# Attention phase of a two-layer encoder step: sinks as a kept PSUM column, first loads in another order, output products one step sooner, values stored by halves

## Chip, cores and metric

The kernel runs on one core of one Trainium2 chip. The metric is the device time of one launch in microseconds (us), as the median of several runs. A profiled execution gives the trace that all durations below come from. The engines are called PE (matrix multiplications), PEld (its weight loads), DVE (vector), ACT (scalar functions), POOL (the fourth compute engine) and SP (which here only issues DMAs).

## Reference

2048 prompt tokens and 32 sampled tokens of width 1024 go through a DeltaNet layer, then through a layer of sliding-window attention with learned sinks. Only the second one is touched by the change, apart from an order of columns.

```python
def sink_softmax(s, sinks):
    sk = sinks.astype(jnp.float32)[..., None, None]
    m = jnp.maximum(s.max(-1, keepdims=True), sk)
    p = jnp.exp(s - m)
    return p / (p.sum(-1, keepdims=True) + jnp.exp(sk - m))

def swa_layer(x, k, v, pos, cached, w_in, sinks, w_out, ln_g, ln_b):
    proj = x @ w_in
    q = rope_partial(proj[..., :B_QW].reshape(b, l, B_Q_HEADS, B_HD), pos) * (B_HD ** -0.5)
    q = q.reshape(b, l, B_KV_HEADS, B_GROUP, B_HD)
    z = proj[..., B_QW:]
    ...
    # 16 query heads, 4 key heads, head size 64; a 64-token chunk sees itself and the two chunks before it
    o = banded_attention(q, k, v, sk)          # scores, sink_softmax, times values
    out = (o * jax.nn.silu(z)) @ w_out
    return layer_norm(DN_ALPHA * x + out, ln_g, ln_b)
```

## The kernel before

The first 1747 us of the trace are the DeltaNet layer, the shared keys and values, and the query and gate projections of the second layer. Large matrix products in fp32 are done as three products of a high and a low part (L79 to L81 for the projections, L1117 to L1119 for the output product: 24 matmuls for half the columns of 128 tokens).

The last 420 us are `Attention.run`. Its instructions stand on PE, DVE, ACT, POOL and SP in the order in which the code writes them (`manual_schedule`), and an engine takes them strictly in that order. `run` goes over the 64-token chunks in the order 14 to 31, then 0 to 13, and then the sampled tokens; i counts the places in that order (0 to 31, `last` = 32 for the sampled ones). Each chunk has two groups of heads, p = 0 and 1. One iteration i does on PE:

- `values(i)`: the probabilities of chunk i times the values, into two PSUM banks (L1701);
- `score(i+2, 0)`: scores of the chunk after next into a PSUM tile S (L1660);
- `turn(i+1, 0)`: transposes of probabilities into the PSUM tile tr (L1683);
- half the output product of the 128-token tile `po` (two chunks make a tile; c says which half of the columns);
- `turn(i+1, 1)` and `score(i+2, 1)`.

The output product uses the banks of `values`, so `values(i+1)` needs the bank that `added` (DVE L1125: residual r plus product) empties. The softmax of one (i, p) is a chain across engines: the largest score (DVE L1480), the sink joined to it (DVE L1483), the sink's difference (DVE L1493), four exps with their sums (ACT L1490) and one of the sink (ACT L1494), the total (DVE L1497), its reciprocal (DVE L1500) and the shares (POOL L1504, two operations in place). ACT (L1689) and DVE (L1690) copy the transposed tile out, and `gated` (DVE L1712) multiplies the result by the gate zs into graw.

A finished tile goes through `finish` (load of the residual r, L1511), `cast` (ACT L1518), `rest` (POOL L1522: the low part), its two products, `stats` (DVE L1538), `norm` (DVE: L1543, L1546, then Newton steps for the inverse root, L484, L487 and three times L491, L493, L495, then L1551), `normed` (ACT L1554), `affine` (POOL L1558 and L1559, 128x1024 each) and `store`. `step(n)` takes n instructions of the norm that is under way and puts them at that place on DVE.

Before the loop and in iterations 0 and 1 the last gate projections are woven in as fills: `gates` yields after each half of a gate, and `fill(n)` takes n of them. They need two weight slabs (`w_raw`, L48; cast on ACT L55, low part on DVE L56), which are fetched while `gates` runs. Up to the end of iteration 1 there is one score tile S; then `opened` frees the projection's memory, a second S tile appears, and the late six of eight output weight slices (`wo`, L1438), the norm's tables, keys and values (`vd`, L1464) of the first chunks are loaded.

Of the kernel before, what the change touches and what calls it, by code (L numbers as in the profile page):

```python
# [22 lines left out]
NP = 2048  # L23
# [1380 lines left out]
class Attention:  # L1404
# [4 lines left out]
    def __init__(self, tc, left, I, O, T, G):  # L1409
# [10 lines left out]
        self.turn = 0  # L1420
# [3 lines left out]
        self.nsk = one.tile([128, 8], F32, tag="nsk", name="nsk")  # L1424
        self.sks = one.tile([128, 4], F32, tag="sks", name="sks")
        for i in range(2):
            nc.sync.dma_start(self.nsk[i * 64:i * 64 + 64, :], I["sinks"][i].partition_broadcast(64))
        for i in range(4):
            nc.sync.dma_start(self.sks[i * 32:i * 32 + 32, :], I["sinks_s"][i].partition_broadcast(32))
        V.tensor_scalar(out=self.nsk[:], in0=self.nsk[:], scalar1=-1.0, scalar2=None, op0=ALU.mult)  # L1430
        V.tensor_scalar(out=self.sks[:], in0=self.sks[:], scalar1=-1.0, scalar2=None, op0=ALU.mult)
# [12 lines left out]
    def open_right(self, right):  # L1444
        tc, I = self.tc, self.I
        R = "right"
        self.oone = new_pool(tc, right, "u_one", 1, side=R)
        self.otwo = new_pool(tc, right, "u_two", 2, side=R)
        self.ps_s.append(new_pool(tc, right, "u_ps", 1, PSUM, side=R))

# [18 lines left out]
    def scores_tile(self):  # L1469
        self.turn += 1  # L1470
        return self.ps_s[self.turn % len(self.ps_s)].tile([128, 2, 2, 256], F32, tag="S", name="S")

    def open_softmax(self, S, P, nskc, whole):

        x = types.SimpleNamespace(S=S, P=P, nskc=nskc, whole=whole, n=len(P))
        x.nm, x.sm, x.es = (self.thr.tile([128, 4], F32, tag=t, name=t)[:, :x.n] for t in ("nm", "sm", "es"))
# [5 lines left out]
    def with_sink(self, x):  # L1482
        self.nc.vector.tensor_tensor(out=x.nm, in0=x.nm, in1=x.nskc, op=ALU.min)  # L1483

    def exps(self, x):
        for u in range(x.n):
            src = x.S[:, u, :]
            if len(x.P[u].shape) == 3:
                src = src.rearrange("r (j k) -> r j k", k=64)
            self.nc.scalar.activation(x.P[u], src, AF.Exp, bias=x.nm[:, u:u + 1], scale=1.0, accum_out=x.sm[:, u:u + 1])  # L1490
# [11 lines left out]
    def shares(self, x):  # L1502
        for P, f in x.whole(x.sm):
            self.nc.gpsimd.tensor_tensor(out=P, in0=P, in1=f, op=ALU.mult)  # L1504
# [84 lines left out]
    def sampled_scores(self, p):  # L1589
        nc, thr = self.nc, self.thr  # L1590
        ks, _, _, qs, _ = self.sampled
        S = self.scores_tile()
# [3 lines left out]
        P = thr.tile([128, 2, 384], F32, tag="P", name="P")  # L1596
        return P, self.open_softmax(
            S[:, :, 0, :160], [P[:, 0, :160], P[:, 1, :160]], self.sks[:, p * 2:p * 2 + 2],
            lambda sm: [(P[:, :, :160], sm[:, 0:2].unsqueeze(2).to_broadcast([128, 2, 160]))])
# [17 lines left out]
    def sampled_values(self, pts):  # L1617
# [3 lines left out]
        ot = self.scores_tile()[:, 0, 0].rearrange("q (h k) -> q h k", h=2)  # L1621
        for p in range(2):
            for half in range(2):
                g = p * 2 + half
# [580 lines left out]
```

## Time and profile before

| | before |
|---|---|
| runs | 2165.35, 2168.01, 2168.23 us |
| median | 2168.01 us |
| profiled execution | 2170.42 us (span 2168.6) |
| mean granted PE clock | 0.993 |
| busy share PE, DVE, ACT, POOL | 97%, 64%, 41%, 38% |
| HBM read, written | 188.58 MB, 116.60 MB |

Times in the timeline rows are microseconds from the start of the span. A row has the start, the duration, the engine, the source line, the operation with its output and inputs, and in brackets the idle time before it with what ended that. A row with x8 stands for eight instructions in a run. Matmuls overlap, so the distance between two starts is the pace, not the duration.

### The profile page before, as it was taken

How to read it: one execution, taken by the hardware profiler on the slowest of the kernel's cores; microseconds unless marked ns; L12 is line 12 of the kernel's file. 1: busy time of each engine (PE TensorE's matmuls, PEld its weight loads, DVE VectorE, ACT ScalarE, POOL GpSimd, SP SyncE). 2: the span in 40 equal slices, each digit the busy share in tenths (PEclk: the TensorE clock that was granted, in tenths of full speed). 3: DMA queues.
4: the chain of work that ended last, by engine and by line, in shares of the span. 5: the costliest groups of instructions: out<-in, count | busy, mean ns of one | idle time of the engine just before them, and what ended most of it. 6: DMA issues, size and time to landing. Idle time of an engine off the chain costs nothing.

```text
span 2168.6 us, 37497 instructions
## 1 busy us (share of the span) xinstructions
PE 2112.2 (97%) x14062; PEld 1936.5 (89%) x14062; DVE 1385.8 (64%) x2717; ACT 892.3 (41%) x2271; POOL 825.6 (38%) x1179
## 2 busy tenths in 40 slices
PE   8999999999999999999999999999999987999997
PEld 6999999999999999999988888999999975777775
DVE  3676666765658578878968885135442234788886
ACT  4444444356522466666742213222112234455541
POOL 1422322212132367767711202056441113556664
PEclk9999999999999999999999999999999998999999
DMA  5213323256575545446847764374221188334311
GB/s 201 69 60 98 110 88 113 71 163 215 159 229 153 172 149 161 155 155 218 272 136 228 227 183 145 96 238 167 71 77 68 67 197 244 91 94 116 98 60 54
DMA packets 267830, 307.28 MB, mean 142 GB/s; under 512 B 79696, under 2 KB 198800, under 8 KB 267376
## 3 DMA queue, kind: packets, MB, share of 16 engines
q1 hardware_dynamic: 256400, 281.40, 41.8%
q10 hardware_dynamic: 11248, 23.48, 3.3%
q8 instruction: 111, 1.82, 0.3%
q14 instruction: 71, 0.58, 0.1%
HBM read 188.58 MB, written 116.60 MB: 141 GB/s over the span
## 4 chain that ended last, share of the span: by engine, by line
PE 86%; DVE 6%; DMA 3%; SPq 2%; ACT 1%; POOL 1%; issue 1%; ACTq 0%; POOLq 0%; DVEq 0%
PE ps L79 17%; PE ps L81 17%; PE ps L80 17%; PE po L1119 3%; PE po L1117 3%; PE po L1118 3%; PE ot L1117 2%; PE ot L1701 2%; PE ot L1119 2%; PE ot L1118 2%; PE S L1660 2%; PE tr L1683 1%; PE ks L817 1%; PE gq L802 1%; PE g L675 1%; DVE nm L1483 1%
## 5 line engine op out<-in xcount | busy, mean ns | idle before, releaser
L79 PE MATMUL ps<-act_hi,w_hi 128*128 128x416 f32 x2000 | 707.1, 354 | 1.6 <-ACT act_hi L70 1.5
L81 PE MATMUL ps<-act_hi,w_lo 128*128 128x416 f32 x2000 | 704.3, 353 | 1.2 <-POOL w_lo L56 1.2
L80 PE MATMUL ps<-act_lo,w_hi 128*128 128x416 f32 x2000 | 701.3, 351 | 0.4 <-DVE act_lo L71 0.4
L79 PEld LDWEIGHTS ps<-act_hi,w_hi 128*128 128x128 f32 x2000 | 376.5, 188 | 8.4 <-ACT act_hi L70 2.2
L80 PEld LDWEIGHTS ps<-act_lo,w_hi 128*128 128x128 f32 x2000 | 376.2, 188 | 5.3 <-DVE act_lo L71 0.9
L81 PEld LDWEIGHTS ps<-act_hi,w_lo 128*128 128x128 f32 x2000 | 375.9, 188 | 5.2 <-POOL w_lo L56 1.7
L56 POOL TENSOR_TENSOR w_lo<-w_raw,w_hi 128x1024 fp32r<-128x1024 f32 x44 | 117.1, 2661 | 473.8 <-ACT w_hi L55 437.8
L209 DVE SCALAR_TENSOR_TENSOR y<-R,convw,y 128x2083 f32<-128x2083 f32 x72 | 183.0, 2542 | 63.0 <-ACT y L206 47.2
L1504 POOL TENSOR_TENSOR P<-P,sm 128x384 f32<-128x384 f32 (+3 forms) x130 | 101.5, 805 | 214.1 <-DVE sm L1500 117.8
L1490 ACT ACTIVATE P<-S,nm 128x192 f32<-128x192 f32 (+2 forms) x260 | 105.1, 425 | 147.0 <-DVE nm L1483 97.5
L709 POOL TENSOR_TENSOR tm<-L,Tt 128x60 f32<-128x60 f32 (+19 forms) x365 | 126.4, 346 | 102.4 <-issue 40.5
L711 POOL TENSOR_TENSOR Tt<-Tt,tm 128x60 f32<-128x60 f32 (+19 forms) x365 | 140.7, 385 | 28.6
L1117 PE MATMUL ot<-wo,g_hi 128*128 128x512 f32 x256 | 103.9, 406 | 1.5 <-DVE graw L1712 1.3
L305 ACT COPY R<-ps 128x416 f32<-128x416 f32 (+1 forms) x144 | 60.3, 442 | 108.3 <-PE ps L81 96.2
L1117 PE MATMUL po<-wo_hi,g_hi 128*128 128x512 f32 x256 | 103.4, 404 | 0.0
L1119 PE MATMUL ot<-wo,g_lo 128*128 128x512 f32 x256 | 101.1, 395 | 0.0
L1118 PE MATMUL ot<-wo,g_hi 128*128 128x512 f32 x256 | 101.1, 395 | 0.0
L1119 PE MATMUL po<-wo_hi,g_lo 128*128 128x512 f32 x256 | 100.2, 392 | 0.6 <-DVE g_lo L1160 0.6
L1315 POOL TENSOR_TENSOR rs<-rs,sin 128x416 f32<-128x416 f32 x50 | 70.7, 1413 | 78.4 <-DVE rs L1314 71.8
L1400 DVE SCALAR_TENSOR_TENSOR za<-zs,za 128x416 f32<-128x416 f32 x40 | 31.7, 796 | 107.5 <-ACT za L1399 104.1
L1118 PE MATMUL po<-wo_lo,g_hi 128*128 128x512 f32 x256 | 99.9, 390 | 0.0
L55 ACT CAST w_hi<-w_raw 128x1024 fp32r<-128x1024 f32 x46 | 48.3, 1050 | 98.7 <-PE ps L80 72.8
(296 smaller groups left out, 3966.9 us busy)
## 6 DMA issues: line engine op xcount, KB each, us to landing
w_raw<-in_w_in SPq DMA_DIRECT2D x40, 512.0 KB
w_raw<-in_b_w_in SPq DMA_DIRECT2D x18, 512.0 KB
k<-s_k SPq DMA_DIRECT2D x17, 512.0 KB
E<-s_E SPq DMA_DIRECT2D x17, 512.0 KB
s_bz<-za SPq DMA_DIRECT2D x40, 208.0 KB
s_bq<-ra SPq DMA_DIRECT2D x40, 208.0 KB
s_q<-y SPq DMA_DIRECT2D x8, 1024.0 KB
s_wo<-wo_parts SPq DMA_DIRECT2D x16, 512.0 KB
```

The source lines that it names most:

```text
L56: sub.tensor_tensor(out=lo[:], in0=raw[:], in1=hi[:], op=ALU.subtract)
L79: nc.tensor.matmul(ps, hi[:, k, :], xh[:, k, :], start=(k == 0), stop=False)
L80: nc.tensor.matmul(ps, hi[:, k, :], xl[:, k, :], start=False, stop=False)
L81: nc.tensor.matmul(ps, lo[:, k, :], xh[:, k, :], start=False, stop=(k == KC - 1))
L209: nc.vector.scalar_tensor_tensor(out=y[:], in0=R[:, j:j + W], scalar=self.convw[:, i, j:j + 1], in1=y[:], op0=ALU.mult, op1=ALU.add)
L709: P.tensor_tensor(out=tm[:n, i0 - k:, :w], in0=L[:n, i0:, j:j + 1].to_broadcast(sh), in1=Tt[:n, j:j + 1, :w].to_broadcast(sh), op=ALU.mult)
L711: P.tensor_tensor(out=Tt[:n, i0:, :w], in0=Tt[:n, i0:, :w], in1=tm[:n, i0 - k:, :w], op=ALU.subtract)
L1117: nc.tensor.matmul(ps[:n], ghi[:, k, :n], hi, start=a, stop=False)
L1118: nc.tensor.matmul(ps[:n], ghi[:, k, :n], lo, start=False, stop=False)
L1119: nc.tensor.matmul(ps[:n], glo[:, k, :n], hi, start=False, stop=z)
L1490: self.nc.scalar.activation(x.P[u], src, AF.Exp, bias=x.nm[:, u:u + 1], scale=1.0, accum_out=x.sm[:, u:u + 1])
L1504: self.nc.gpsimd.tensor_tensor(out=P, in0=P, in1=f, op=ALU.mult)
```

## The change

Four things change, all in the attention phase.

*Sinks.* The sink's value stands in a PSUM column of its own behind the 192 scores (column n-1), written by ACT's `place_sinks` (L1477) only when that column would move: eight times at the start, later at the wrap of the order and for the sampled tokens, 16 copies in all. The largest score and the four exps run over 193 columns, so the separate sink operations (DVE L1483, L1493, L1497 and ACT L1494) are gone. The exps write a tile e, and the shares (now L1510) read e and write P. After `opened` the second score tile S gets its sinks before `score(3, 1)`.

*Loads.* The fetch of the first woven weight slab stands right behind the first queries; the gates' zs of the first chunks come last. At `opened` the residual r of the first tile is loaded ahead of the output weights. Values are kept in another column order, so `vd` is loaded by two DMAs with longer runs instead of four.

*Products.* The first output product stands in iteration 3 instead of 4, c is `(i + 1) % 2`, and the code behind the loop has half a tile's product less and begins with the sampled tokens' values.

*Norm.* The norm of a tile begins in an odd iteration, with five Newton steps after the second reciprocal, and goes on in the next. Its `normed` and `affine` stand in the odd iteration after that, behind the shares, while the next tile's norm begins. Before, they stood at the end of the odd iteration that ended the norm.

On DVE, in an iteration in which a norm begins (before: even i, after: odd i), these rows stand from the second softmax's end to the copy that follows the iteration's last transposes. Before (sm is the sum, es the sink's exp, ln_t and ln_y the norm's Newton values, r the residual, ot the product's bank, tr the transposed tile):

```order
L484 TENSOR_SCALAR ln_y<-ve 128x1
L1500 RECIPROCAL sm<-sm 128x4
L487 TENSOR_SCALAR ln_y<-ln_y 128x1
L491 SCALAR_TENSOR_TENSOR ln_t<-ve,ln_y 128x1
L493 TENSOR_TENSOR ln_t<-ln_t,ln_y 128x1
L495 SCALAR_TENSOR_TENSOR ln_y<-ln_t,ln_y 128x1
L1497 TENSOR_TENSOR sm<-sm,es 128x4
L491 SCALAR_TENSOR_TENSOR ln_t<-ve,ln_y 128x1
L1500 RECIPROCAL sm<-sm 128x4
L1125 SCALAR_TENSOR_TENSOR r<-r,ot 128x512
L1690 COPY pt<-tr 128x384
```

Between the two reciprocals stand the first Newton round and one step of the second, and L1125 comes straight after the second reciprocal. The same place of the program after, on the same engine:

```order
L484 TENSOR_SCALAR ln_y<-ve 128x1
L487 TENSOR_SCALAR ln_y<-ln_y 128x1
L1500 RECIPROCAL sm<-sm 128x4
L491 SCALAR_TENSOR_TENSOR ln_t<-ve,ln_y 128x1
L493 TENSOR_TENSOR ln_t<-ln_t,ln_y 128x1
L495 SCALAR_TENSOR_TENSOR ln_y<-ln_t,ln_y 128x1
L491 SCALAR_TENSOR_TENSOR ln_t<-ve,ln_y 128x1
L493 TENSOR_TENSOR ln_t<-ln_t,ln_y 128x1
L1125 SCALAR_TENSOR_TENSOR r<-r,ot 128x512
L1691 COPY pt<-tr 128x384
```

Five Newton steps now stand between the second reciprocal and L1125; in before there was none there. On POOL, the order is the same in both (two sets of shares, the low part, two sets of shares, the two affine rows), so what moved is DVE's part against it.

On SP, at the start of the phase, the difference runs from the keys to the second slab (s_bq, s_bz and s_bv are the queries, gates and values in memory):

```order
-L1456 DMA kT<-s_bk 128x2x384
-L1642 DMA qs<-s_bq 128x8x64 x2
-L1643 DMA zs<-s_bz 128x8x128
-L1464 DMA vd<-s_bv 64x6x64 x4
-L1642 DMA qs<-s_bq 128x8x64 x2
-L1643 DMA zs<-s_bz 128x8x128
-L48 DMA w_raw<-in_b_w_in 128x1024
+L1457 DMA kT<-s_bk 128x2x384
+L1647 DMA qs<-s_bq 128x8x64 x2
+L48 DMA w_raw<-in_b_w_in 128x1024
+L1463 DMA vd<-s_bv 64x6x128 x2
+L1647 DMA qs<-s_bq 128x8x64 x2
+L1652 DMA zs<-s_bz 128x8x128 x2
```

The slab moved ahead of zs, vd, the second qs and the second zs. On SP at `opened`, after:

```order
L1647 DMA qs<-s_bq 128x8x64 x2
L1520 DMA r<-s_h 128x1024
L1438 DMA wo<-s_wob 128x2x1024 x6
L1099 DMA ln_g<-in_b_ln_g 128x1024
L1100 DMA ln_b<-in_b_ln_b 128x1024
L1457 DMA kT<-s_bk 128x2x768
L1463 DMA vd<-s_bv 64x12x128 x2
L1652 DMA zs<-s_bz 128x8x128
```

Before, r (L1511) stood last here, behind vd, and zs stood behind qs.

The core of the diff:

```diff
     def load_values(self, a, z):
-        src = self.T["bv"][0:NP, :].rearrange("(c k) (p d) -> k c p d", k=64, p=2)
+        src = self.T["bv"][0:NP, :].rearrange("(c k) (h x) -> k c h x", k=64, h=2)
         for i in range(2):
-            rows = slice(i * 64, i * 64 + 64)
-            for p in range(2):
-                self.nc.sync.dma_start(self.vd[rows, a:z, p, :], src[:, a:z, p, rows])
+            self.nc.sync.dma_start(self.vd[i * 64:i * 64 + 64, a:z].rearrange("k c p d -> k c (p d)"), src[:, a:z, i])
...
+    def place_sinks(self, p, units, n, sinks):
+
+        i = p % len(self.S)
+        if self.held.get(i) != (n, sinks):
+            self.held[i] = n, sinks
+            src = self.sinks[:, sinks:sinks + 2 * units].rearrange("r (h u) t -> r h u t", h=2)
+            self.nc.scalar.copy(self.S[i][:, :, :units, n - 1:n + 1], src)
...
-    def with_sink(self, x):
-        self.nc.vector.tensor_tensor(out=x.nm, in0=x.nm, in1=x.nskc, op=ALU.min)
...
-    def sink_exp(self, x):
-        self.nc.vector.tensor_tensor(out=x.es, in0=x.nm, in1=x.nskc, op=ALU.subtract)
-        self.nc.scalar.activation(x.es, x.es, AF.Exp)
-
-    def total(self, x):
-        self.nc.vector.tensor_tensor(out=x.sm, in0=x.sm, in1=x.es, op=ALU.add)
...
     def shares(self, x):
-        for P, f in x.whole(x.sm):
-            self.nc.gpsimd.tensor_tensor(out=P, in0=P, in1=f, op=ALU.mult)
...
+        for u in range(units):
+            self.nc.gpsimd.tensor_tensor(
+                out=x.P[:, u, :nj * 128].rearrange("r (j h k) -> r j h k", h=2, k=64),
+                in0=x.e[:, :, u, :n].rearrange("r h (j k) -> r j h k", k=64),
+                in1=x.sm[:, :, u].unsqueeze(1).unsqueeze(3).to_broadcast([128, nj, 2, 64]), op=ALU.mult)
...
-        fill(3)
+        sinks(0, 0)
+        fill(4)
         early(0, 0)
...
-        fill(1)
-        po = following = stored = None
+        po = done = following = stored = None
         for i in range(last):
-            c = i % 2
-            if c == 0:
-                if i >= 4:
-                    done, po = po, following
+            c = (i + 1) % 2
+            if i >= 3 and c == 0:
+                done, po = po, following
...
-            if lean:
-                largest(i + 2, 0)
-                shares(i + 1, 1)
-                copies(i + 1, 0)
-                exps(i + 2, 0)
-            else:
-                copies(i + 1, 0)
-                largest(i + 2, 0)
-                exps(i + 2, 0)
+            copies(i + 1, 0)
+            largest(i + 2, 0)
+            exps(i + 2, 0)
+            shares(i + 1, 1)
             if i < 2:
                 fill(2)
             if po:
                 self.product(po, c, 0)
-            if i >= 5:
+            old = None
+            if i >= 4:
                 x = po if c else done
                 if x:
                     self.stats(x, 1 - c)
                     if c == 0:
+                        old = norm[0]
+                        step(20)
                         norm[:] = x, self.norm(x)
-            step(2)
-            if not lean:
-                shares(i + 1, 1)
             step(4)
             shares(i + 2, 0)
-            if c == 0 and i >= 2:
-                following = self.finish(*self.pend.pop(0))
+            step(5)
+            if c == 1 and i >= 2:
+                if i > 2:
+                    following = self.finish(*self.pend.pop(0))
                 self.cast(following)
                 self.rest(following)
-            if c == 1 and norm[0]:
-                step(20)
-                self.normed(norm[0])
-                self.affine(norm[0])
-                stored, norm[0] = norm[0], None
-            if c == 0 and stored:
+            if old:
+                self.normed(old)
+                self.affine(old)
+                stored = old
+            elif stored:
                 self.store(stored)
                 stored = None
...
             if i == 1:
                 self.start(order[6])
-                opened()
+                following = opened()
+                self.gate(order[6])
+                sinks(3, 1)
             score(i + 2, 1)
-        done, po = po, following
-        self.product(po, 0, 0)
-        self.stats(done, 1)
         self.store(stored)
-        norm[:] = done, self.norm(done)
-        step(3)
+        old = norm[0]
+        step(20)
+        self.normed(old)
         self.pend.append(self.sampled_values(got(last)))
         final, sampled = self.pend
-        self.product(po, 0, 1)
+        self.product(po, 1, 0)
...
     def opened():
         right.close()
         att.open_right(right)
+        first = att.finish(*att.pend.pop(0))
         att.load_late()
         att.load_keys(0, 12)
         att.load_values(0, 12)
+        return first
 
     with tc.manual_schedule(engines={ET.PE, ET.DVE, ET.Activation, ET.Pool, ET.SP}):
         att.load_keys(12, 18)
         att.start(14)
+        raw = fetch_weights(nc, p2.wp, I["b_w_in"][12])
         att.load_values(12, 18)
         att.start(16)
-        att.run(gates(), opened)
+        att.gate(14)
+        att.gate(16)
+        att.run(gates(raw), opened)
```

More of the change, by code (lines that the diff above doesn't have):

```diff
@@ L1661, in scores @@
                                  self.kT[hs, p, kc0 * 64:kc0 * 64 + nk], start=True, stop=True)
[L1662 to L1671 removed]
+        x = self.open_softmax(S[:, :, :, :nk + 1])
+        return x.P, x
     def turned(self, n, P):
@@ L1771, in step @@
         def step(n):
-            for _ in range(n):
-                if norm[1]:
-                    if next(norm[1], 0) == 0:
-                        norm[1] = None
+            for _ in range(n if norm[1] else 0):
+                next(norm[1], None)
         def early(i, p):
@@ L1874, in run @@
         self.rest(some)
-        step(20)
-        self.normed(done)
-        self.affine(done)
-        self.added(po, 0)
-        self.stats(po, 0)
-        self.product(po, 1, 0)
+        self.affine(old)
         self.product(po, 1, 1)
+        self.added(po, 1)
+        self.stats(po, 1)
         end = self.finish(*final)
@@ L1884, in run @@
         self.rest(end)
-        self.store(done)
-        self.added(po, 1)
-        self.stats(po, 1)
+        self.store(old)
+        drain(self.norm(po))
+        self.normed(po)
+        self.affine(po)
         for c in range(2):
@@ L1890, in run @@
             self.product(some, c, 1)
-            if c == 0:
-                drain(self.norm(po))
-                self.normed(po)
-                self.affine(po)
             self.added(some, c)
```

128 lines of the change are left out of this document (64 added, 64 removed).

## The prediction

> **What bounds the kernel now.** I read the page first: its busy line and its chain of waits.
>
> ```profile
> PE 2112.2 (97%) x14062; PEld 1936.5 (89%) x14062; DVE 1385.8 (64%) x2717; ACT 892.3 (41%) x2271; POOL 825.6 (38%) x1179
> PE 86%; DVE 6%; DMA 3%; SPq 2%; ACT 1%; POOL 1%; issue 1%; ACTq 0%; POOLq 0%; DVEq 0%
> ```
>
> PE is busy or is the chain nearly all the time, so an edit pays only where it closes a gap of PE, or moves PE work into one. The change touches only the attention phase, the last 420 us; the earlier phases differ by a permutation of w_v's columns alone. Then the windows (columns: stretch, its length, busy time of PE, PEld, DVE, ACT and POOL, granted clock, DMA share, GB/s), cut where values(0), values(2), values(5) and values(31) start on PE; the three others are iterations 7, 11 and 12.
>
> ```profile
> 1747.00:1777.40 30.40, 24.08 (x130) 21.60 (x130) 10.83 (x22) 10.81 (x37) 4.83 (x6) 0.89 1.03 239
> 1801.30:1837.26 35.96, 24.06 (x182) 16.52 (x180) 17.07 (x47) 15.18 (x62) 15.88 (x16) 0.88 1.00 313
> 2115.65:2168.60 52.95, 41.49 (x202) 29.64 (x200) 32.34 (x97) 9.42 (x18) 25.82 (x13) 0.95 0.15 55
> 1859.92:1870.14 10.22, 10.22 (x79) 7.82 (x77) 7.73 (x22) 5.50 (x21) 6.20 (x7) 1.00 0.37 104
> 1902.91:1913.41 10.50, 10.49 (x79) 7.86 (x77) 8.26 (x23) 5.50 (x21) 6.50 (x7) 1.00 0.32 100
> 1913.41:1924.62 11.21, 10.64 (x78) 7.75 (x76) 10.14 (x24) 5.31 (x21) 6.88 (x6) 1.00 0.39 95
> ```
>
> Three stretches hold PE's idle time: the start (6.3 us), iterations 2 to 4 (11.9) and the tail (11.5). In the steady part an iteration takes 10.22 us when PE never waits, and a pair of them now takes 10.50 + 11.21 = 21.71. The PE timeline names the gaps (idle time and its releaser in brackets).
>
> ```profile
> 1747.03 0.92 PE L1660 MATMUL S<-kT,qs 64*128 64x192 f32 x8 [1.45 <-DMA qs<-s_bq]
> ...
> 1764.59 1.65 PE L1660 MATMUL S<-kT,qs 64*128 64x192 f32 x8 [6.29 <-ACT P L1490]
> ...
> 1770.29 0.37 PE L81 MATMUL ps<-act_hi,w_lo 128*128 128x416 f32 x1
> ...
> 1773.32 0.82 PE L1683 MATMUL tr<-ident,P 128*128 128x128 f32 x6
> ...
> 1776.54 0.35 PE L81 MATMUL ps<-act_hi,w_lo 128*128 128x416 f32 x1
> ...
> 1781.97 0.92 PE L1660 MATMUL S<-kT,qs 64*128 64x192 f32 x8 [0.59 <-ACT P L1490]
> ...
> 1810.59 1.84 PE L1701 MATMUL ot<-pt,vd 64*64 64x256 f32 x24
> ...
> 1837.26 2.84 PE L1701 MATMUL ot<-pt,vd 64*64 64x256 f32 x24 [7.24 <-DVE r L1125]
> ...
> 1849.70 1.53 PE L1701 MATMUL ot<-pt,vd 64*64 64x256 f32 x24
> ```
>
> After the 6.29 us wait PE is also slow: scores, transposes and eight gate matmuls take from 1764.59 to 1770.29, 5.70 us, and the same set later from 1773.32 to 1776.54, 3.22. That wait costs 2.48 us more than it shows. The timelines of ACT, DVE and SP give the causes.
>
> ```profile
> 1752.13 1.22 SPq L48 DMA_DIRECT2D w_raw<-in_b_w_in  x1
> 1759.10 1.04 ACT L55 CAST w_hi<-w_raw 128x1024 fp32r<-128x1024 f32 x1 [7.24 <-DMA w_raw<-in_b_w_in]
> 1804.22 4.17 SPq L1438 DMA_DIRECT2D wo<-s_wob  x6
> 1830.35 0.96 SPq L1511 DMA_DIRECT2D r<-s_h  x1
> 1836.52 0.69 DVE L1125 SCALAR_TENSOR_TENSOR r<-r,ot 128x512 f32<-128x512 f32 x1 [9.44 <-DMA r<-s_h]
> ```
>
> The weight slab w_raw is issued behind two rounds of attention loads and lands 7 us later; ACT's cast waits for it, and the second exps are queued behind the cast. In iteration 4 the residual r is issued 26 us after the output weights and the sum L1125 waits for it, which keeps values(5) waiting for its bank.
>
> **The change part by part.** *Start, to values(2).* The slab is fetched right behind the first qs and ahead of vd, the second qs and zs, so SP issues it earlier than at 1752.13 by the time of eight loads; if that is 7.24 us or more, ACT's wait goes, and with it PE's 6.29 and the slow 2.48. I count it whole; each us short of that would leave a us. One more gate half stands ahead of the first scores (fill(4)), covering the 1.45; the 0.59 before S at 1781.97 goes with the shorter softmax chain. What comes in: S(3,1) writes a bank in which ACT has first to place the sink column, behind the exps before it. No row shows this wait; it lies between 0 and a set of four exps (1.7 us, below), and I take 0.9. Sum: −1.45 −6.29 −2.48 −0.59 +0.9 = **−9.9**. The loads put behind the slab are needed at values(0), 25 us on, so their delay costs nothing; vd in two DMAs instead of four takes SP time that nobody waits for.
>
> *Iterations 2 to 4.* At the opening r now goes first, so the 7.24 us before values(5) go. But products start at i=3, one iteration sooner: 24 matmuls of output product come into a stretch where PE waited, and need all eight weight slices. The sizes, from the DMA issues (KB each):
>
> ```profile
> wo<-s_wob SPq DMA_DIRECT2D x6, 1024.0 KB
> r<-s_h SPq DMA_DIRECT2D x3, 512.0 KB
> qs<-s_bq SPq DMA_DIRECT2D x8, 256.0 KB
> ```
>
> Ahead of the last slice stand 2 qs, r and 6 wo, 7 MB. At this stretch's 313 GB/s that is 22.4 us, and about 2 to begin: 24.4 after the opening (the end of iteration 1). PE wants it 1.8 us (to values(2)) + 9.3 (values(2) to values(3), 1801.32 to 1810.59) + 3.1 (values, scores and transposes of iteration 3) + 4.9 (seven eighths of the product) = 19.1 after it. Wait: 5.3; from 410 GB/s on there would be none; I take 3, nearer to what this stretch shows. So i=2 stays 9.3, i=3 is 10.22 + 3, i=4 10.22 with 0.5 for a slow clock behind the wait: 33.2 against 35.96, **−2.7**, with half a tile's product more done.
>
> *The steady part.* Removed in each of the 66 softmaxes: three DVE operations of 0.16 and an ACT one. Off the critical path mostly, but one of the three is what stalls the pair now. The rows:
>
> ```profile
> 1915.27 2.37 POOL L1559 TENSOR_TENSOR r<-r,ln_b 128x1024 f32<-128x1024 f32 x1
> 1915.33 2.33 DVE L1483 TENSOR_TENSOR nm<-nm,nsk 128x4 f32<-128x4 f32 x1
> ...
> 1921.08 0.18 DVE L1500 RECIPROCAL sm<-sm 128x4 f32<-128x4 f32 x1
> 1921.37 0.16 DVE L491 SCALAR_TENSOR_TENSOR ln_t<-ve,ln_y 128x1 f32<-128x1 f32 x1
> 1921.42 1.61 POOL L1504 TENSOR_TENSOR P<-P,sm 128x384 f32<-128x384 f32 x2 [3.78 <-DVE ln_y L487]
> 1921.56 0.70 DVE L493 TENSOR_TENSOR ln_t<-ln_t,ln_y 128x1 f32<-128x1 f32 x1
> 1922.30 0.75 DVE L495 SCALAR_TENSOR_TENSOR ln_y<-ln_t,ln_y 128x1 f32<-128x1 f32 x1
> ...
> 2122.95 2.40 POOL L1558 TENSOR_TENSOR r<-r,ln_g 128x1024 f32<-128x1024 f32 x1 [0.59 <-ACT r L1554]
> 2124.50 0.69 DVE L1125 SCALAR_TENSOR_TENSOR r<-r,ot 128x512 f32<-128x512 f32 x1 [2.91 <-PE ot L1119]
> ```
>
> L1483, with 4 columns, takes 2.33 us because it starts while POOL's affine row runs and ends with it. The 128x1 Newton steps (L491, L493, L495; 0.16 each alone) take 0.70 and 0.75 beside POOL's two share operations of 0.8: an operation that reads two SBUF operands gets in only at a boundary between two POOL operations, one per boundary. L1125, which reads one of its tensors from PSUM, keeps its 0.69 beside a POOL row. [...]
>
> For in after, the affine of the old tile stands on POOL right behind shares(i+2,0) in the iteration (odd i, from 7) in which DVE runs five Newton steps of the next tile ahead of L1125. I place them by these rows, from the start of values(i):
>
> ```profile
> 1859.92 1.53 PE L1701 MATMUL ot<-pt,vd 64*64 64x256 f32 x24
> 1863.61 0.95 DVE L1480 TENSOR_REDUCE nm<-S 128x4 f32<-128x768 f32 x1
> 1864.85 0.43 ACT L1490 ACTIVATE P<-S,nm 128x192 f32<-128x192 f32 x1
> 1866.54 1.26 ACT L1554 ACTIVATE r<-r,nb,ln_y 128x1024 f32<-128x1024 f32 x1
> ```
>
> The reduce of (i+2,0) ends 4.64 in; the four exps take 1.7 (1864.85 to 1866.54, where ACT goes on to its next work) and the reciprocal comes about 0.2 behind, T = 6.5. By the 1921 rows POOL's shares start at T+0.34 and end at T+1.96. The first L491 (T+0.10) and L493 (T+0.29) pass; L495 gets in at the boundary between the shares, the second L491 at their end. ACT's pass over the old tile (1.26 from T) is done, so POOL goes straight on to its first affine row, and the second L493 waits for the end of that: T+4.31 = 10.8. L1125 (0.69) then ends at 11.5 to 11.6, and values(i+1), which writes the bank that L1125 empties, starts about 0.07 later, 11.64, where PE would have been ready at 10.22. So an odd iteration costs 11.64 and an even one, now without L1483's stall, 10.22: 21.86 a pair against 21.71. Between values(5) and values(31): i=5 gains 2.2 (12.44 before, 1837.26 to 1849.70, with a slow clock behind the wait), i=7 loses 1.4, twelve even ones gain 1.0 each, eleven odd ones lose 1.14 each: **−0.3**. If the order bites once more or not at all, that is the first or second rival.
>
> *Tail.* The half product done at i=3 leaves it.
>
> ```profile
> 2118.60 0.50 PE L1117 MATMUL ot<-wo,g_hi 128*128 128x512 f32 x1 [0.68 <-DVE graw L1712]
> ...
> 2124.07 0.39 PE L1119 MATMUL ot<-wo,g_lo 128*128 128x512 f32 x1
> ```
>
> 24 matmuls from 2118.60 on, at 0.233 each, are 5.6 us; the 0.68 ahead of them goes as well, since what follows the loop no longer starts with that product. The last odd iteration's stall shows here: +1.5. **−4.8**.
>
> Sum: −9.9 −2.7 −0.3 −4.8 = −17.7. The profiled execution took 2170.42 (span 2168.6 and 1.8 around it), 2.4 above the median shown; after it should read 2152.7, and the median 2168.01 − 17.7 = 2150.3, say **2150**. With both ends of the wait at i=3 and of S(3,1), and 0.5 us either way per odd iteration, this case alone spans 2142 to 2160.
>
> **The rivals.** (1) *The order bites twice, and the kernel gets slower.* POOL starts its shares 0.05 us before the place where L493 ran. If shares start earlier by that or more, or one of L491/L493 comes later, every later step moves back one boundary, and the last stands behind the second affine row: +2.4 for each of the 13 odd iterations from 7 to 31, +31: 2181. The point is whether the first L493 starts before or after POOL. Against it: the 1921 pattern, with this distance, is the same in all twelve pairs of the trace. For it: shares now read rows of 193 from another tile, and the margin is thin. A wait that long may also drop the clock as after 6.29 us, up to 2200. [...] Chance 0.15.
> (2) *No lock that matters*: the Newton steps get in between, or normed ends later than I place it. Each of 13 odd iterations then has 10.22: −18.5, 2132. For it: only one row's place decides. Against it: POOL has nothing to wait for. Chance 0.12.
> (3) *Output weights take the place of r*: if the queue runs at the 239 GB/s of the first window, 7 MB need 29.3 + 2, a wait of 12.2 instead of 3: +9, 2159. For it: that stretch also has stores and small rows beside it. Against it: those end before the opening. Chance 0.13.
>
> **How the numbers follow.** My forecast has 0.58; 0.02 is left for what I have not seen. Predicted 2150. The range takes in the main case, (3) and just (2), 2131 to 2167, and leaves out (1). A measurement of this kernel can tell 0.2%, 4.3 us, from no change. Below 2163.7 lie nearly all of the main case, (2) and most of (3): faster 0.80. Same 0.05, slower 0.15.
>
> **What would show it.** Right: no PE wait over 1 us before S(1,0) and the cast of w_hi without a wait for w_raw; no wait for r; a wait of 0 to 5 us for wo in iteration 3; odd iterations of 11.6 with one Newton step of about 2.3 us under the first affine row, even ones of 10.22; a tail of about 48. Odd iterations of 14 with a step under the second affine row mean (1), all at 10.22 mean (2), over 8 us of wo wait mean (3). The sum is wrong if another releaser than these stands at a PE gap over 1 us.

## The result, and the profile after

| | before | after |
|---|---|---|
| median, range | 2167.12 us (2165.35 to 2168.23) | 2152.41 us (2150.35 to 2153.83) |
| ratio, 95% interval | | 0.9932 (0.9915 to 0.9949) |
| profiled execution, span | 2170.42, 2168.6 | 2153.83, 2151.6 |

The kernel is faster by 14.7 us. The page of after, busy line and chain:

```profile
PE 2100.6 (98%) x14062; PEld 1934.8 (90%) x14062; DVE 1353.2 (63%) x2518; ACT 893.0 (42%) x2221; POOL 828.3 (38%) x1179
PE 88%; DVE 5%; DMA 3%; issue 2%; ACT 2%; POOL 0%; SPq 0%; ACTq 0%; DVEq 0%; POOLq 0%
```

PE runs the same 14062 matmuls; DVE has 199 instructions fewer. The windows of after, cut at the same events as before (values(0) to values(2), iteration 3, values(5) to values(31), the tail, and one even and one odd iteration):

```profile
1764.70:1789.03 24.33, 23.53 (x178) 20.13 (x176) 9.97 (x22) 11.97 (x46) 6.94 (x9) 1.00 0.56 177
1798.44:1817.14 18.70, 14.41 (x79) 9.58 (x77) 4.66 (x9) 4.40 (x18) 4.66 (x5) 0.77 1.04 393
1827.96:2105.29 277.33, 262.86 (x1934) 201.13 (x1932) 206.29 (x442) 137.57 (x497) 167.68 (x141) 1.00 0.33 92
2105.29:2151.60 46.31, 35.62 (x178) 24.92 (x176) 31.53 (x86) 9.10 (x16) 23.14 (x11) 0.94 0.18 63
1881.69:1891.93 10.24, 10.24 (x76) 7.88 (x76) 7.02 (x16) 5.22 (x19) 6.46 (x6) 1.00 0.40 104
1891.93:1903.45 11.52, 10.30 (x78) 7.82 (x76) 9.29 (x19) 5.53 (x19) 7.01 (x7) 1.00 0.28 92
```

To compare starts, the two traces are laid on one gate matmul that stands ahead of the whole phase in both programs, the 60th L79 from the last:

```profile
1740.88 0.35 PE L79 MATMUL ps<-act_hi,w_hi 128*128 128x416 f32 x1
```

```profile
1738.87 0.35 PE L79 MATMUL ps<-act_hi,w_hi 128*128 128x416 f32 x1
```

The first row is of before, the second of after. After is 2.0 us earlier here already, in work that the change does not touch, so 2.0 of the 17.0 between the two spans is no effect of the change. (In the traces of the experiments below, whose earlier phases are those of after, it starts between 1737.92 and 1740.47.) The other 15.0 agree with the 14.7 of the medians.

| stretch | forecast | measured | before and after |
|---|---|---|---|
| that matmul to values(2) | -9.9 | -10.3 | 60.44, 50.16 |
| values(2) to values(5) | -2.7 | +3.0 | 35.95, 38.93 |
| values(5) to values(31) | -0.3 | -1.1 | 278.39, 277.33 |
| values(31) to the end | -4.8 | -6.7 | 52.98, 46.30 |
| sum | -17.7 | -15.1 | |

The PE timeline of after shows what is left of the gaps, with the releaser in brackets:

```profile
1788.18 0.92 PE L1669 MATMUL S<-kT,qs 64*128 64x192 f32 x8 [0.80 <-ACT S L1477]
...
1794.81 0.47 PE L1684 MATMUL tr<-ident,P 128*128 128x128 f32 x1 [2.60 <-POOL P L1510]
...
1807.57 0.50 PE L1117 MATMUL ot<-wo,g_hi 128*128 128x512 f32 x1 [1.09 <-DMA wo<-s_wob]
...
1810.14 0.50 PE L1117 MATMUL ot<-wo,g_hi 128*128 128x512 f32 x1 [1.60 <-DMA wo<-s_wob]
...
1812.70 0.79 PE L1117 MATMUL ot<-wo,g_hi 128*128 128x512 f32 x1 [1.59 <-DMA wo<-s_wob]
...
1859.92 1.55 PE L1702 MATMUL ot<-pt,vd 64*64 64x256 f32 x24 [1.22 <-DVE r L1125]
```

The 6.29 us before S(1,0), the wait for qs and the 7.24 us for r before values(5) are gone; 0.80 for the sink copy before S(3,1) is new, as are the waits for output weights. The 2.60 for POOL's shares in iteration 2 stood before as well (2.02). From 1859.92 on, one wait of 1.22 for L1125 stands in every pair (1.56 and 0.72 once each instead). SP and ACT of after show why the start is free: the slab is issued 8 us earlier (1741.82 against 1752.13, less the 2.0) and the cast waits for nothing.

```profile
1741.82 1.59 SPq L48 DMA_DIRECT2D w_raw<-in_b_w_in  x1
1750.30 1.05 ACT L55 CAST w_hi<-w_raw 128x1024 fp32r<-128x1024 f32 x1
```

DVE and POOL of after, in an odd iteration:

```profile
1876.73 0.18 DVE L1500 RECIPROCAL sm<-sm 128x4 f32<-128x4 f32 x1 [0.45 <-POOL P L1510]
1876.83 0.13 DVE L491 SCALAR_TENSOR_TENSOR ln_t<-ve,ln_y 128x1 f32<-128x1 f32 x1
1876.99 0.16 DVE L493 TENSOR_TENSOR ln_t<-ln_t,ln_y 128x1 f32<-128x1 f32 x1
1877.08 1.62 POOL L1510 TENSOR_TENSOR P<-e,sm 128x384 f32<-128x384 f32 x2 [0.42 <-DVE ln_t L491]
1877.19 0.74 DVE L495 SCALAR_TENSOR_TENSOR ln_y<-ln_t,ln_y 128x1 f32<-128x1 f32 x1
1877.96 0.76 DVE L491 SCALAR_TENSOR_TENSOR ln_t<-ve,ln_y 128x1 f32<-128x1 f32 x1
1878.66 2.36 POOL L1567 TENSOR_TENSOR r<-r,ln_g 128x1024 f32<-128x1024 f32 x1
1878.75 2.29 DVE L493 TENSOR_TENSOR ln_t<-ln_t,ln_y 128x1 f32<-128x1 f32 x1
1880.96 0.68 DVE L1125 SCALAR_TENSOR_TENSOR r<-r,ot 128x512 f32<-128x512 f32 x1
1881.10 2.35 POOL L1568 TENSOR_TENSOR r<-r,ln_b 128x1024 f32<-128x1024 f32 x1
```

Two steps pass, one gets in between the shares, one at their end, and the fifth (L493, 2.29 us for a column) ends with the first affine row; L1125 stands behind it. The pair takes 10.24 + 11.52 = 21.76 where 21.86 was forecast.

### The profile page after: what moved, and what is told of

It reads as the page before. It is cut to its first block, busy times and chain, and to the rows that moved or that the text cites. A ratio compares the mean times of both kernels' runs of the same rounds, so it can differ in the third digit from the quotient of the medians.

```text
span 2151.6 us, 37233 instructions
## 1 busy us (share of the span) xinstructions
PE 2100.6 (98%) x14062; PEld 1934.8 (90%) x14062; DVE 1353.2 (63%) x2518; ACT 893.0 (42%) x2221; POOL 828.3 (38%) x1179
## 4 chain that ended last, share of the span: by engine, by line
PE 88%; DVE 5%; DMA 3%; issue 2%; ACT 2%; POOL 0%; SPq 0%; ACTq 0%; DVEq 0%; POOLq 0%
PE ps L79 17%; PE ps L81 17%; PE ps L80 17%; PE po L1119 3%; PE po L1117 3%; PE po L1118 3%; PE ot L1702 2%; PE S L1669 2%; PE ot L1117 2%; PE ot L1119 2%; PE ot L1118 2%; PE tr L1684 2%; PE g L675 1%; PE ks L817 1%; PE gq L802 1%
## 5 line engine op out<-in xcount | busy, mean ns | idle before, releaser
L79 PE MATMUL ps<-act_hi,w_hi 128*128 128x416 f32 x2000 | 706.9, 354 | 0.9 <-ACT act_hi L70 0.9
L79 PEld LDWEIGHTS ps<-act_hi,w_hi 128*128 128x128 f32 x2000 | 376.4, 188 | 6.9 <-ACT act_hi L70 1.5
L1510 POOL TENSOR_TENSOR P<-e,sm 128x384 f32<-128x384 f32 (+2 forms) x128 | 101.1, 811 | 197.9 <-DVE sm L1500 183.6
L1496 ACT ACTIVATE e<-S,nm 128x193 f32<-128x193 f32 (+2 forms) x260 | 104.6, 415 | 115.8 <-DVE nm L1491 76.5
```

The lines of the kernel that those rows point to most:

```text
L79: nc.tensor.matmul(ps, hi[:, k, :], xh[:, k, :], start=(k == 0), stop=False)
L1496: self.nc.scalar.activation(x.e[:, h, u, :x.n], x.S[:, h, u, :], AF.Exp, bias=x.nm[:, h, u:u + 1], scale=1.0, accum_out=x.sm[:, h, u:u + 1])
L1510: self.nc.gpsimd.tensor_tensor(out=x.P[:, u, :nj * 128].rearrange("r (j h k) -> r j h k", h=2, k=64), in0=x.e[:, :, u, :n].rearrange("r h ...
```

## The experiments

All are edits of the kernel after, whose median was 2152.4; each median below is over four runs (ten for e5 and e7). The ratios are to before, which was run again beside each experiment (medians 2166.16 to 2167.63), so a difference of 1 us from after is within what such a repetition moves.

**How many Newton steps stand behind the second reciprocal.** The edits change one number; steps not taken here go to the next iteration. "Lock" in the expectations is a name for what the rows of after show: Newton steps on DVE with two SBUF operands, 0.16 us each when nothing runs beside them, took 0.74 and 0.76 beside POOL's shares and 2.29 under its first affine row, and ended with those operations of POOL.

```diff
-            step(5)
+            step(5 if c else 2)        # e1; 4 in e12, 6 in e2, 7 in e10
```

e1, two steps. 

> The kernel after, with two Newton steps instead of five behind the second reciprocal of an odd iteration; the other three move into the next iteration, where nine places are free. Theory (lock): L491 and L493 pass ahead of POOL's shares, nothing stands between them and L1125, so no DVE step waits for an affine row. Odd iterations go from 11.51 to about 10.25 us, thirteen of them: -16, so about 2136. Rival (queue length: L1125 is late only because five operations stand ahead of it): three fewer operations at 0.19 give -0.6 for each, -8 in all, about 2144, and the odd iterations still 10.9. Rival (the wait only moves: the deferred steps meet POOL's shares and the low part in the even iteration): odd 10.25, even 11.5, about 2152.

e12, four steps. 

> The kernel after, with four Newton steps instead of five behind the second reciprocal of an odd iteration. Theory (lock, boundary by boundary): L491 and L493 pass, L495 gets in between the shares and the second L491 at their end; the step that ended with the first affine row is the fifth, so without it L1125 is not held and odd iterations take 10.23, as with two steps: about 2138. Rival (each step costs its part of the 1.3 us): odd iterations 11.1 to 11.3, about 2148.

e2, six steps. 

> The kernel after, with six Newton steps instead of five behind the second reciprocal of an odd iteration: one operation of 0.16 us more. Theory (lock, one two-operand DVE operation per boundary between POOL operations): the sixth step stands behind the second affine row, so L1125 and the values that follow come 2.4 us later, odd iterations about 13.9 instead of 11.5, +31, about 2183, more if PE's clock drops in the longer wait. Rival (queue length): +0.2 for each odd iteration, +3, about 2155.

e10, seven steps. 

> The kernel after, with seven Newton steps behind the second reciprocal of an odd iteration. Six_steps showed that the sixth step still gets in between the two affine rows, because the second row, which needs the first one's output, begins some 0.08 us after it. Theory (lock): the seventh comes too late for that gap, ends with the second affine row and holds L1125: odd iterations go to about 13.9, +30 against the kernel after, about 2183, more if PE's clock drops. Rival (queue length): +0.2 for each odd iteration again, about 2159.

| steps | median | ratio, 95% interval | odd, even iteration |
|---|---|---|---|
| 2 | 2137.72 | 0.9863 (0.9848 to 0.9877) | 10.23, 10.23 |
| 4 | 2137.69 | 0.9865 (0.9849 to 0.9882) | 10.23, 10.23 |
| 5 (after) | 2152.41 | 0.9932 (0.9915 to 0.9949) | 11.51, 10.25 |
| 6 | 2156.23 | 0.9950 (0.9935 to 0.9965) | 11.75, 10.23 |
| 7 | 2200.37 | 1.0146 (1.0131 to 1.0162) | 13.93, 10.23 to 13.07 |

The time goes in steps, not in proportion to the operations. Four cost as little as two, the fifth costs 1.28 us in each odd iteration, the sixth 0.24, the seventh 2.18 more. That L1125 is late only because more operations stand ahead of it (the rival of queue length) falls as an explanation. With four steps, DVE and POOL show that nothing is held:

```profile
1876.52 0.76 DVE L491 SCALAR_TENSOR_TENSOR ln_t<-ve,ln_y 128x1 f32<-128x1 f32 x1
1877.56 0.69 DVE L1125 SCALAR_TENSOR_TENSOR r<-r,ot 128x512 f32<-128x512 f32 x1 [0.28 <-PE ot L1119]
```

L1125 now waits for PE's product, and PE for nothing. For six steps I had forecast a loss of 31 us, and 4 came. Its rows show why:

```profile
1876.45 2.28 DVE L493 TENSOR_TENSOR ln_t<-ln_t,ln_y 128x1 f32<-128x1 f32 x1
1878.76 0.16 DVE L495 SCALAR_TENSOR_TENSOR ln_y<-ln_t,ln_y 128x1 f32<-128x1 f32 x1
1878.79 2.36 POOL L1568 TENSOR_TENSOR r<-r,ln_b 128x1024 f32<-128x1024 f32 x1
```

The second affine row reads what the first wrote and starts 0.08 us after its end (1876.36 + 2.35 to 1878.79). The held L493 ends at 1878.73, and L495 starts at 1878.76, 0.03 before POOL. So at this boundary two operations got through. Between the shares, and between them and the first affine row, POOL goes on without a gap (the shares run from 1874.78 for 1.62, the affine row starts at 1876.36), and it was one. That the dependence of the second row makes the gap is argued from its 0.08 us; nothing else was tried. The seventh step then comes too late, as expected of e10, and ends with the second affine row:

```profile
1884.85 2.34 POOL L1568 TENSOR_TENSOR r<-r,ln_b 128x1024 f32<-128x1024 f32 x1
1885.01 2.19 DVE L491 SCALAR_TENSOR_TENSOR ln_t<-ve,ln_y 128x1 f32<-128x1 f32 x1
1887.12 0.68 DVE L1125 SCALAR_TENSOR_TENSOR r<-r,ot 128x512 f32<-128x512 f32 x1
```

The rest of its loss, 2200 instead of 2183, is a slow PE clock behind the longer waits (3.63 us where after has 1.22): even iterations of up to 13.07 with nothing new to do, and a mean granted clock of 0.985 against 0.996.

**e3, no affine in the loop.**

```diff
                 self.normed(old)
-                self.affine(old)
                 stored = old
```

> The kernel after, with the affine (two POOL operations of 128x1024) left out in the loop; the five Newton steps stay where they are. What is stored lacks gain and bias. Theory (lock): the second L493 waits only for the shares' end, L1125 ends about 9.3 into the iteration, no stall, odd iterations about 10.25, about 2136. Rival (queue length, or the steps' own latency): odd iterations stay 11.5, about 2152.

2137.55 us (0.9864, 0.9850 to 0.9879), odd iterations 10.23. All five steps stand where they stood, and without POOL's two rows they cost nothing. Together with e12, which keeps the affine and takes one step away (odd iterations 10.23 as well), this shows that neither the step nor the affine costs by itself here: the pair of them does (11.51).

**e4, tables, keys and values later; e9, weight slices first.** Both concern the wait for output weights in iteration 3.

```diff
 # e4: at the opening, only the weights; the rest at the start of iteration 4
-        att.load_keys(0, 12)
-        att.load_values(0, 12)
...
+            if i == 4:
+                self.load_rest()       # ln_g, ln_b
+                self.load_keys(0, 12)
+                self.load_values(0, 12)
 # e9: at the opening
-                self.start(order[6])
                 following = opened()
...
-        first = att.finish(*att.pend.pop(0))
...
         self.w += self.weights(self.oone, self.EARLY, KC)
+        self.first_r = self.finish(*self.pend.pop(0))
+        self.start(20)
```

> The kernel after, with the norm's tables and the first chunks' keys and values (3 MB that are needed only from iteration 7 and 16 on) issued at the start of iteration 4 instead of behind the output weights. Theory (shared DMA engines): in the kernel after these loads run beside the last output weight slices and take a share of the 400 GB/s; without them the product of iteration 3, which now takes 11.4 us instead of 5.6, takes 7 to 9, iteration 3 goes from 18.7 to 14 to 16.5, total 2148 to 2150. Rival (the slices come one after the other and the loads behind them don't matter): product 11.4, total 2152.

e4: 2153.03 us (0.9933, 0.9917 to 0.9950), no change. Its PE rows have the slices as far apart as before, although the tables are now issued only at 1815.62:

```profile
1808.95 0.50 PE L1117 MATMUL ot<-wo,g_hi 128*128 128x512 f32 x1 [1.59 <-DMA wo<-s_wob]
...
1811.51 0.80 PE L1117 MATMUL ot<-wo,g_hi 128*128 128x512 f32 x1 [1.59 <-DMA wo<-s_wob]
...
1814.14 0.80 PE L1117 MATMUL ot<-wo,g_hi 128*128 128x512 f32 x1 [0.98 <-DMA wo<-s_wob]
```

```profile
1815.62 1.02 SPq L1099 DMA_DIRECT2D ln_g<-in_b_ln_g  x1
```

2.56 us for 1 MB is 410 GB/s, in this kernel as in after (1810.14 to 1812.70), and the last slice is there 23.6 us after values(2) starts, in after 23.7. My theory, that loads behind the slices share the engines with them, fell: the slices come one behind the other. What is left is what stands ahead of them, which e9 changes.

> The kernel after, with the six late output weight slices first in SP's queue when the second half's memory opens, then r, then the queries of iteration 6, then the tables (in the kernel after: queries, r, slices). Late_rest showed that slices land 2.56 us apart whatever stands behind them. Theory (a queue served in order: what stands ahead of the slices counts): the queries and r take 3 to 4 us ahead of them; every slice lands 3 to 4 earlier, the product of iteration 3 takes 8 instead of 11.4, iteration 3 about 15 instead of 18.7, total about 2149. Rival (the slices can't begin earlier, since memory frees late): 2152.

e9: 2146.88 us (0.9898, 0.9881 to 0.9914), 5.5 less than after. The waits for wo that are left in its PE timeline:

```profile
1805.23 0.50 PE L1117 MATMUL ot<-wo,g_hi 128*128 128x512 f32 x1 [0.66 <-DMA wo<-s_wob]
1807.78 0.79 PE L1117 MATMUL ot<-wo,g_hi 128*128 128x512 f32 x1 [1.59 <-DMA wo<-s_wob]
```

The last slice is there at 1807.78 instead of 1812.70, 4.9 us sooner, and values(2) to values(5) takes 32.75 us instead of 38.93. That is even 0.45 below my forecast for after (33.2). What left its place ahead of the slices (two loads of queries and r) is 1 MB, 2.56 us at the pace of the slices; SP also issues the slices 3.5 us sooner, as the rows of after and then of e9 show:

```profile
1792.30 3.59 SPq L1438 DMA_DIRECT2D wo<-s_wob  x6
```

```profile
1788.82 4.75 SPq L1438 DMA_DIRECT2D wo<-s_wob  x6
```

Part of the 38.93 is scatter: in the traces of e1, e2, e3, e10 and e12, which leave these iterations as they are in after, the stretch takes 37.2 to 38.3 us, and the last slice is there 21.9 to 23.4 us after values(2) starts, against 18.7 in e9.

**e5, the slab fetched late.**

```diff
-        raw = fetch_weights(nc, p2.wp, I["b_w_in"][12])
+        att.gate(14)
         att.load_values(12, 18)
         att.start(16)
-        att.gate(14)
         att.gate(16)
+        raw = fetch_weights(nc, p2.wp, I["b_w_in"][12])
```

> The kernel after, with the first woven weight slab fetched where it stood before (behind zs, vd, the second qs and zs). Theory: ACT's cast again waits for w_raw, the second exps stand behind it, and PE's wait of about 6.3 us before S(1,0) is back with the slow clock of 2.5 behind it: +8.8, about 2161. Rival (the early part of the gain came from the shorter softmax and fill(4), not from the slab): within 2 us of 2152.

2163.67 us (0.9979, 0.9970 to 0.9988): 11.3 of the 14.7 are lost, 2.5 more than expected. The start explains 8.8 in the profiled execution (58.98 against 50.16), as forecast. Further on in that execution values(2) to values(5) gives back 3.0, where values(2) starts 8.8 later but the last weight slice is there only 7.0 later, and iterations 13 and 14 together cost 3.45. These two nearly cancel, so where the other 2.5 of the median come from stays open. PE and ACT:

```profile
1762.56 1.65 PE L1669 MATMUL S<-kT,qs 64*128 64x192 f32 x8 [5.93 <-ACT S L1477]
```

```profile
1756.75 1.04 ACT L55 CAST w_hi<-w_raw 128x1024 fp32r<-128x1024 f32 x1 [6.78 <-DMA w_raw<-in_b_w_in]
```

The wait and the slow clock (1.65 for the scores that take 0.92) are back. In iteration 13 of the same execution something else happened, which the prediction's first rival had described:

```profile
1926.01 1.62 POOL L1510 TENSOR_TENSOR P<-e,sm 128x384 f32<-128x384 f32 x2 [0.42 <-DVE sm L1500]
1926.04 0.81 DVE L491 SCALAR_TENSOR_TENSOR ln_t<-ve,ln_y 128x1 f32<-128x1 f32 x1 [0.20 <-DVE sm L1500]
...
1930.18 2.19 DVE L493 TENSOR_TENSOR ln_t<-ln_t,ln_y 128x1 f32<-128x1 f32 x1
```

L491 began 0.03 us after POOL instead of 0.25 before it, as in the rows of after above. So L491 and L493 were held too, every step moved back, the fifth ended with the second affine row, and that iteration took 13.93 us with an even one of 11.60 behind it. The five-step order is as near to this as 0.25 us.

**e7, the old sink operations put back into each softmax.**

```diff
     def largest(self, x):
         self.nc.vector.tensor_reduce(out=x.nm, in_=x.S, axis=AX.X, op=ALU.max, negate=True)
+        self.nc.vector.tensor_tensor(out=x.nm, in0=x.nm, in1=x.nm, op=ALU.min)
...
+        self.nc.vector.tensor_tensor(out=x.es, in0=x.nm, in1=x.nm, op=ALU.subtract)
+        self.nc.scalar.activation(x.es, x.es, AF.Exp)
...
     def inverse(self, x):
+        self.nc.vector.tensor_tensor(out=x.sm, in0=x.sm, in1=x.es, op=ALU.max)
         self.nc.vector.reciprocal(out=x.sm, in_=x.sm)
```

> The kernel after, with operations of the old form and place added to every softmax: a minimum of nm with itself (DVE), a difference and its exp (DVE, ACT), a maximum of sm with that exp (DVE); the result stays the same. Theory: in odd iterations the chain to the second reciprocal, which L1125 hangs on, gets about 0.5 us longer (three DVE operations of 0.16 and the ACT one of 0.2, part of it hidden), +0.5 for each of thirteen: +6.5, about 2159; even iterations have room. Rival (they are hidden): 2152. Rival (the lock): the minimum, two operands from SBUF, stands about 1.1 us into the even iteration under the second affine row, holds the exps and the next reduce and costs over 1 us for each pair: 2165 or more.

2166.12 us (0.9995, 0.9985 to 1.0006): 13.7 lost, twice what I expected. Odd iterations take 12.12, 0.61 more for a forecast of 0.5. The even ones have two values: 11.85 up to iteration 14, 10.23 from iteration 20 on. PE's rows after two odd iterations, and the windows behind them (the granted clock is the third number from the right):

```profile
1881.63 2.61 PE L1706 MATMUL ot<-pt,vd 64*64 64x256 f32 x24 [1.83 <-DVE r L1125]
...
2063.20 1.55 PE L1706 MATMUL ot<-pt,vd 64*64 64x256 f32 x24 [1.83 <-DVE r L1125]
```

```profile
1881.00:1893.00 12.00, 11.37 (x72) 8.65 (x74) 8.58 (x23) 5.53 (x21) 5.71 (x6) 0.86 0.37 90
2062.00:2075.00 13.00, 11.80 (x102) 8.81 (x102) 10.82 (x26) 5.42 (x21) 8.30 (x7) 1.00 0.28 77
```

Behind the same wait of 1.83 us the granted clock is 0.86 in the first of these windows and 1.00 in the second. So in this order the sink's operations cost 0.6 in each odd iteration, and in this trace about as much again at the lower clock; in after, where a wait of 1.22 is left, the granted clock is 1.00 from values(5) to values(31). The ten runs lie between 2162.24 (mean granted clock 0.995) and 2172.05 us (0.991), so this part varies from run to run. The minimum is held too, the third possibility, but that costs little: where it is held it takes 0.33 to 0.63, once 0.99, instead of 0.16.

```profile
1870.63 0.62 DVE L1492 TENSOR_TENSOR nm<-nm 128x4 f32<-128x4 f32 x1
```

**e6, values by four DMAs.**

```diff
-            self.nc.sync.dma_start(self.vd[i * 64:i * 64 + 64, a:z].rearrange("k c p d -> k c (p d)"), src[:, a:z, i])
+            for p in range(2):
+                self.nc.sync.dma_start(self.vd[i * 64:i * 64 + 64, a:z, p, :], src[:, a:z, i, p * 64:p * 64 + 64])
```

> The kernel after, with the values loaded by four DMAs with 256-byte runs instead of two with 512. Theory: nobody waits for these loads, and those at the opening stand behind the output weights: 2152 within 2. Rival (the shorter runs hold the DMA engines while the weight slices are under way): the product of iteration 3 later by 1 us or more, 2154 or more.

2153.15 us (0.9937, 0.9922 to 0.9952), not to be told from after. In the one trace the start takes 1.9 us longer (52.09), and in it ACT waits for a store of gates, which SP issues behind these loads, and the exps stand behind it on ACT:

```profile
1758.33 0.52 ACT L1399 ACTIVATE za<-ps 128x416 f32<-128x416 f32 x1 [1.23 <-DMA s_bz<-za]
```

Whether the loads delayed the store, and whether that is so in every run, stays open.

**e11, two steps and weight slices first.** The edits of e1 and e9 together.

> The kernel after, with two Newton steps behind the second reciprocal and the six output weight slices first in the queue at the opening. Theory: two causes in two places, so the gains add: 2152.4 - 14.7 - 5.5 = 2132. Rival (they overlap): 2136 or more.

2130.95 us (0.9840, 0.9825 to 0.9854): 21.5 less than after, 35 less than before. The gains add (14.7 and 5.5 make 20.2). In its trace one wait of 0.64 for wo is left.

## Why the prediction was right

The total came out at 2152.4 for a forecast of 2150.3, with the 14.7 measured for 17.7 forecast. The stretch that was mis-sized by 5.7 is made up in part by the other three, which gained 0.4, 0.8 and 1.9 more than forecast; that they cancel about half of it is luck.

*Start, right.* -10.3 for -9.9; the sink copy costs 0.80 for 0.9. e5 shows that 8.8 of it hang on the slab.

*Iterations 2 to 4, mis-sized by 5.7.* Two terms of the sum were too small, the 3 us for the wait at i=3 and the 0.5 for a slow clock behind it.

With the 3 us the last weight slice would have been there 20.3 us after values(2) starts. It was there after 23.7 (1789.03 to 1812.70), 3.4 later. I had taken a value between 0 and 5.3 without a row for it, and nearer to 5.3 would have been right. The 5.3 is itself too small: it counts 7 MB as 7.0 million bytes, and with 7.34 million the same sum at 313 GB/s gives 6.3, and a last slice after 23.6. That this meets the 23.7 is partly luck, since the first load of the opening was issued 0.3 us ahead of values(2) and not 1.8. The about 2 us to begin in that sum were an estimate of mine that no run shows; what the trace of before shows is 1.6 us from the issue of the last load of sks, 0.5 KB at 1741.7, to DVE's L1431 at 1743.33, which waited for it. In PE's rows the wait is the three of 1.09, 1.60 and 1.59.

Behind the last slice, iterations 3 and 4 took 15.3 us where I had 12.9, with the 0.5 for the clock in it: a slow clock of 2.9 (granted 0.81 from 1812.70 to 1827.96). The transposes of iteration 3 took 1.48 and the scores 1.65 there, for 0.82 and 0.92 later. The slow clock ahead of the last slice hardly counts, because PE has to wait for the slice anyway: in e10 iteration 2 took 8.12 us instead of the 9.41 of after, where the granted clock was 0.79 (e9 took 8.20 at 1.00), but iteration 3 then took 19.32 instead of 18.69, and the last slice was there 0.7 sooner.

One of the signs that the prediction had named for a wrong sum showed, a PE gap over 1 us with another releaser: the 2.60 for POOL's shares in iteration 2. It lies inside the 9.3 us that the forecast took over from before, and the iteration took 9.41, so the miss is not there. My third rival, this wait at 239 GB/s, was right in kind and too large in size.

*Steady part, right in mechanism and size.* The forecast loss of 1.42 in an odd iteration is 1.28, with a wait of 1.22; e12 and e3 show its cause, and e10 its next step. A stalled pair takes 21.76, as much as before (21.71): the one stalled step of before (L1483, 2.33) was exchanged for another (L493, 2.29).

*Tail, 1.9 too small a gain.* The product and the gap left it as forecast (6.3). The 1.5 for a stall behind the last odd iteration did not come: the Newton steps are held there too (2.23 for an L495), but nothing of PE hung on them.

*First rival.* Its price was right where its condition holds, as in iteration 13 of e5, and its condition was put too widely. A slip of one step costs 0.24 (e2), since two operations passed between the affine rows there; only where both the first L491 and the first L493 miss their place does it come to the 2.4. e10, in which the last step stands behind the second affine row in each odd iteration, took 2200.4, as its "up to 2200" with a slow clock had it. Its sentence on the margin is the wrong way round: by the prediction's own sum L493 starts 0.05 us ahead of POOL (T+0.29 against T+0.34), and in the rows of after it is 0.09. The bounds given for the main case add up to 2140 to 2160, not 2142 to 2160.

## What to carry over

In this kernel a Newton step on DVE that takes 0.16 us alone took 2.29 under an affine row of POOL. So it paid here to count which two-operand DVE operations come between POOL's operations and to move the small ones ahead of POOL's start or behind its long rows: four steps instead of five took 15 us off a kernel of 2150. In the load queue of this kernel, what stood ahead of the tensor that was waited for counted in full (3 to 5 us for 1 MB and its issue), and moving away what stood behind it brought nothing that could be measured. Where two bounds for a cost come from rows, the row of the same stretch was the better guess here than a value between them. The 1 MB of a slice is 1.05 million bytes, and a sum with GB/s has to count those.

## What the runs showed of the hardware

Behind a wait of 1.83 us PE's clock was lower in some places of one execution, e7, and not in others (values at 2.61 us against 1.55, granted clock 0.86 against 1.00). In after the values behind the waits of 1.22 took 1.55 each time, and behind those of 0.95 to 1.81 in e2 no iteration was slow. Of the twelve waits of 3.1 to 4.0 in e10, eleven are followed by a slow iteration (granted clock 0.77 to 0.88) and one, of 3.63, is not (1.00). Behind a wait of 2.60 in iteration 2 the clock was lower in after and not in e9 (granted 0.79 and 1.00 in that iteration), as the transposes behind it show, first after, then e9:

```profile
1795.60 1.33 PE L1684 MATMUL tr<-ident,P 128*128 128x128 f32 x5 [0.31 <-POOL P L1510]
```

```profile
1795.67 0.76 PE L1686 MATMUL tr<-ident,P 128*128 128x128 f32 x5 [0.46 <-POOL P L1512]
```

What decides whether the clock falls was not tried.

At a boundary between two POOL operations one held DVE operation with two SBUF operands passed where the second followed without a gap (the shares of after from 1877.08 for 1.62, its first affine row from 1878.66), and two where the second, which reads what the first wrote, began 0.08 us later (the affine rows of e2; in e5 it is 0.08 and in e10 0.09, with two as well). The prediction's "one per boundary" was right in these rows for the first kind alone.
